# Rows of a mixture of experts: products with selection matrices, or indirect transfers through memory

## The chip, the core and the metric

The kernel runs on one core of one Trainium2 chip. The metric is device microseconds from start to end of one execution; where several executions are given, their median. TensorE (PE) multiplies, VectorE (DVE) and ScalarE (ACT) work elementwise, GpSimd (POOL) does a little of both, and SyncE (SP) only issues transfers between memory (DRAM) and the on-chip SBUF. Each engine has a queue of its own that it works through in order; semaphores hold an instruction until what it needs has been done. Results of TensorE lie in PSUM.

## What is computed

Two layers on 256 tokens of width 1024: layer 0 is a state-space mixer with memory attention and a dense gated feed-forward, layer 1 an RWKV mixer with memory attention and then the experts, to which the change belongs. Of the reference only these lines matter (8 experts, each token goes to the 2 best, 3584 feed-forward columns an expert):

```python
logits = (hf @ w_router).astype(f32) + b_router.astype(f32)
top_logit, top_idx = lax.top_k(logits, TOP_K)
top_w = jax.nn.softmax(top_logit, axis=-1)
...
xb = hf[row_tok].reshape(n_blocks, MOE_BLOCK, d)
def expert_block(args):
    xblk, e = args
    return swiglu(xblk, w_gate[e], w_up[e], w_down[e])
yb = lax.map(expert_block, (xb, block_expert)).reshape(n_rows, d)
yb = yb * row_w[:, None].astype(yb.dtype)
out = jnp.zeros_like(hf).at[row_tok].add(yb)
```

So each expert takes the rows of its tokens, runs silu(x·gate) · (x·up) through down, and its rows are weighted and added to the tokens that they came from.

## The kernel before

**Precision.** Every large product is made of three fp32r products (`mm3`, L191 to L195): a matrix is split into a high part (ScalarE casts it, `wsh`, L187) and a residual (VectorE subtracts, `wsl`, L188); the same goes for the other factor (`xeh` and `xel`, `ath` and `atl`).

**Experts.** `experts` (L1709) runs 8 experts × 7 chunks of 512 feed-forward columns. A chunk loads three weight pieces of 2 MB (gate, up, down) on SyncE's queue into a ring of 7 buffers. `split` cuts each into 4 pieces of 128x1024; high parts and residuals go through rings of 4. `gate_up` (L1636) makes 24 products of 128x512 for gate and 24 for up into PSUM tiles `gu`, then `sg`: silu on ScalarE (L1649), times up on VectorE (L1650). `act_T` (L1653) turns sg with four transposes into a PSUM tile `t` and splits it into ath (L1658) and atl (L1659). `down` adds 24 products to the expert's sums `yac`. The tiles `t` share a ring of two PSUM buffers, whether sg, an expert's rows or the small products of `back` stand in them:

```python
def tr():
    return pp.tile([P, 4, P], F32, name="t", tag="tr", bufs=2)
def gu():
    return pp.tile([P, 512], F32, name="gu", tag="gu", bufs=4)
```

**Gather and return.** An expert has at most 128 rows here. `Gm` (L1454) is a 0/1 matrix, tokens by places. `rows` multiplies it with the normalised tokens `xhp` (high and low: eight products, L1458); ScalarE copies the result (`xr`, L1465), eight transposes put it in columns (L1468), and `xeh`, `xel` (L1470, L1471) are its parts. `back` (L1476) transposes Gm (L1478), gets each row's weight with two small products (L1480) and copies both. After the last chunk of an expert, `combine` (L1677) scales yac by the weight (yeh on ScalarE, L1685; yel on VectorE, L1686), returns the rows by eight products with the transposed Gm (L1691, L1692) and adds to `xs` (L1696). A gather is written behind chunk 3 of the expert before it, a return between gate and up of chunk 1 of the next. The last return ends the kernel together with the final norm. A second pass for experts with more than 128 rows stands in the program behind a branch and isn't entered here.

**Order.** A scheduler sets the order of the instructions on each engine when the program is built; on the chip each engine keeps to it.

**Elsewhere.** At the start SyncE loads the tokens, the first projection weights and the small matrices of the state-space mixer, `bnat` and `cnat` among them. Before the experts, the router (`xg`, L1570, GpSimd multiplies tokens by the norm's gain into one of two buffers) makes xhp, and `wt`, for each token and expert its weight and its norm factor.

## Time and profile before

| | us |
|---|---|
| median of 3 runs (1590.15 to 1592.48) | 1592.29 |
| the profiled execution | 1590.0 |
| its span | 1588.0 |
| TensorE busy in the span | 1516.3 (95%) |
| VectorE busy | 1283.0 (81%) |
| ScalarE busy | 1073.0 (68%) |
| GpSimd busy | 157.7 (10%) |

The experts take the stretch from about 590 to 1575 us; all that stands before them (two mixers, the dense feed-forward, the router) takes the first 590. Shares over the whole span mix these. The trace can be asked for a stretch (how long each engine is busy in it, at which granted clock of TensorE, at which share of the transfer engines), for lines (how often, how long, what ended the idle time before), and for single instructions in order of time. In such a row the arrow in brackets names the instruction whose end released the one shown, with the idle time ahead of it. PEld is the weight load of TensorE, which runs beside its products. Products overlap, so the price of one is the distance to the next, not the duration in its row.

### The profile page before, as it was taken

To read this page: it belongs to the slowest core of one execution; us is meant where nothing else is said; L and a number is where in the kernel's file an instruction comes from. 1 tells how busy PE (TensorE), PEld (TensorE's weight loads), DVE (VectorE), ACT (ScalarE), POOL (GpSimd) and SP (SyncE) were. 2 spreads that over 40 slices of the span, in tenths; PEclk is the share of its full clock that TensorE was granted. 3 is DMA by queue.
4 is the path that set the end of the run, shared out by engine and by line. 5 is a ranking of instruction groups with operands and counts; after the bars stand their busy time and mean duration, and the time that the engine had idled before them with its cause. 6 is when DMAs were issued, how large, how long until landed. Compare 5 with 4: busy or idle time off the path is not lost. (4 is left out here: it accounts for less than half of the span.)

```text
span 1588.0 us, 21853 instructions
## 1 busy us (share of the span) xinstructions
PE 1516.3 (95%) x8465; PEld 1272.1 (80%) x8465; DVE 1283.0 (81%) x1583; ACT 1073.0 (68%) x1355; POOL 157.7 (10%) x215
## 2 busy tenths in 40 slices
PE   7898999998969889999999999999999999999996
PEld 6776888878958768888888888888888888888885
DVE  7964654546895669899899899899899898988987
ACT  6655544436533348788777777787787887777775
POOL 3451000003652230000000000000000000000000
PEclk9999999999989979999999999999999999999999
DMA  7116553623400958999999999999999999999970
GB/s 202 45 45 237 185 203 117 248 79 94 120 14 22 339 218 313 341 371 359 346 374 353 344 376 356 340 378 356 347 372 363 348 366 361 352 348 366 360 280 29
DMA packets 198031, 423.46 MB, mean 267 GB/s; under 512 B 13952, under 2 KB 35614, under 8 KB 197918
## 3 DMA queue, kind: packets, MB, share of 16 engines
q1 hardware_dynamic: 195746, 419.29, 72.8%
q10 hardware_dynamic: 2172, 2.68, 0.6%
q8 instruction: 68, 1.11, 0.3%
q14 instruction: 45, 0.37, 0.1%
HBM read 420.91 MB, written 1.05 MB: 266 GB/s over the span
## 5 line engine op out<-in xcount | busy, mean ns | idle before, releaser
L188 DVE TENSOR_TENSOR wsl<-w,wsh 128x1024 fp32r<-128x1024 f32 (+1 forms) x757 | 893.8, 1216 | 150.9 <-ACT wsh L187 139.8
L187 ACT CAST wsh<-w 128x1024 fp32r<-128x1024 f32 (+1 forms) x757 | 783.3, 1049 | 250.9 <-PE gu L195 97.1
L194 PE MATMUL gu<-wsl,xeh 128*128 128x512 f32 x896 | 350.7, 391 | 0.0
L193 PE MATMUL gu<-wsh,xeh 128*128 128x512 f32 x896 | 348.9, 396 | 1.6 <-DVE xs L1696 1.6
L195 PE MATMUL gu<-wsh,xel 128*128 128x512 f32 x896 | 349.5, 390 | 0.0
L193 PEld LDWEIGHTS gu<-wsh,xeh 128*128 128x128 f32 x896 | 168.8, 188 | 37.4 <-ACT wsh L187 2.4
L195 PEld LDWEIGHTS gu<-wsh,xel 128*128 128x128 f32 x896 | 168.6, 188 | 35.1 <-DVE xel L1471 0.2
L194 PEld LDWEIGHTS gu<-wsl,xeh 128*128 128x128 f32 x896 | 168.7, 188 | 35.0
L194 PE MATMUL yac<-wsl,ath 128*128 128x512 f32 x440 | 173.0, 393 | 0.0
L195 PE MATMUL yac<-wsh,atl 128*128 128x512 f32 x440 | 171.7, 390 | 0.0
L193 PE MATMUL yac<-wsh,ath 128*128 128x512 f32 x440 | 136.3, 391 | 0.0
L278 POOL TENSOR_TENSOR rs<-vv,mhalf 128x1 f32<-128x1 f32 x8 | 4.4, 557 | 1203.6 <-DVE vv L277 1203.6
L195 PEld LDWEIGHTS yac<-wsh,atl 128*128 128x128 f32 x440 | 82.7, 188 | 17.1
L193 PEld LDWEIGHTS yac<-wsh,ath 128*128 128x128 f32 x440 | 82.2, 188 | 16.9
L194 PEld LDWEIGHTS yac<-wsl,ath 128*128 128x128 f32 x440 | 82.8, 188 | 15.4
L193 PE MATMUL mm<-wsh,hTh 128*128 128x512 f32 (+1 forms) x192 | 71.1, 374 | 0.0
L194 PE MATMUL mm<-wsl,hTh 128*128 128x512 f32 (+1 forms) x192 | 70.8, 371 | 0.0
L195 PE MATMUL mm<-wsh,hTl 128*128 128x512 f32 (+1 forms) x192 | 70.3, 372 | 0.0
L1658 ACT CAST ath<-t 128x512 fp32r<-128x512 f32 x55 | 32.3, 587 | 31.0 <-PE yac L194 30.2
L1650 DVE TENSOR_TENSOR sg<-sg,gu 128x512 f32<-128x512 f32 x56 | 38.1, 681 | 13.7 <-PE gu L195 13.7
L195 PE MATMUL dn<-hTh,wsC 128*128 128x256 f32 x160 | 46.5, 291 | 1.0 <-POOL wsC L1148 0.9
L193 PE MATMUL dn<-hTh,wsC 128*128 128x256 f32 x160 | 46.1, 288 | 0.0
(533 smaller groups left out, 2059.1 us busy)
## 6 DMA issues: line engine op xcount, KB each, us to landing
w<-in_moe_w_gate_dram SPq DMA_DIRECT2D x55, 2048.0 KB
...
```

The source lines that it names most:

```text
L187: S.copy(hv, src)
L188: (eng or V).tensor_sub(lv, src, hv.bitcast(F32))
L193: TE.matmul(ps, xp[0], wh, start=start, stop=False, skip_group_check=True)
L194: TE.matmul(ps, xp[0], wl, start=False, stop=False, skip_group_check=True)
L195: TE.matmul(ps, xp[1], wh, start=False, stop=stop, skip_group_check=True)
L278: hold.append(G.tensor_tensor(rs, vv, mhalf, op=OP.pow).ins)
L1650: V.tensor_mul(sg, sg, ps[1])
L1658: S.copy(at[0], t)
```

## The change

Two buffers in memory are added: `xd`, the 256 tokens' rows, and `yd`, two rows of results for each token. yd is filled with zeros at the start by four writes of 512 KB on SyncE. The router writes each of the four xg to xd (256 KB each). `wt` gets two more columns, the token's number and the number of its row in yd (a token's first expert writes the first half, its second one the second; where the token isn't the expert's, the number lies outside).

For experts 1 to 7 `found` replaces `gather`, one chunk earlier: Gm, the two small products (now four columns: weight, norm factor, token, place), two conversions to integers (`it`), and an indirect transfer on GpSimd's queue that fetches 128 rows of 4 KB from xd into the tile `ye`, of which there is one. Behind chunk 3 the transposes take their rows from ye. For experts 0 to 6 `combine` scales yac into ye (two operations on ScalarE) and an indirect transfer on GpSimd's queue writes the rows to their places in yd; places outside are skipped. In the last expert, behind chunks 2 to 5, `added` loads a quarter of yd into ye (512 KB on SyncE) and VectorE adds it to xs (128x1024). The first expert's gather and the last one's return stay products.

```diff
     consts = pool(ctx, "consts", 1)
-    pad(consts, 64)
     sml = pool(ctx, "sml", 2)
...
     ring = {}
+    dr = pool(ctx, "dr", 1, space=bass.MemoryType.DRAM)
+    xd = dr.tile([T, D], F32, name="xd")
+    yd = dr.tile([2 * T, D], F32, name="yd")
     keep_st = ctx.enter_context(ExitStack())
...
             dma(srow2[:, j, :], a[nm][0].rearrange("(q g) j -> q (g j)", g=8))
+        for i in range(2 * NH):
+            dma(yd[i * P:(i + 1) * P, :], KD_[:, 0:2].rearrange("p q d c -> p (q d c)"))
         bnat = su.tile([P, 2, NST, 16], F32, name="bnat", tag="n1")
...
     xhp = mkpair(mcon, [P, NH, D], "xhp")
-    wt = mcon.tile([P, NH, E, 2], F32, name="wt")
+    wt = mcon.tile([P, NH, E, 4], F32, name="wt")
+    tok = mcon.tile([P, NH], F32, name="tok")
     rs3 = mcon.tile([P, NH], F32, name="rs3")
...
     cmi = mcon.tile([P, 1], I32, name="cmi")
+    pad(mcon, 96)
...
             self.Gm = self.mp.tile([P, NH, P], F32R, name="Gm")
-            self.pg = [pg() for _ in range(2)]
+            self.pg = pg and [pg() for _ in range(2)]
...
                 x_ = xr(q)
-                (V.tensor_copy if q and xrV else S.copy)(x_, self.pg[q])
+                if self.pg:
+                    (V.tensor_copy if q and xrV else S.copy)(x_, self.pg[q])
                 t = self.tr()
...
-        def back(self, tr):
-            self.GT = self.mp.tile([P, NH, P], F32R, name="GT")
+        def back(self, tr, turned):
             t, e = tr(), self.e
+            if turned:
+                self.GT = self.mp.tile([P, NH, P], F32R, name="GT")
+                for h in range(NH):
+                    TE.transpose(t[:, h, :], self.Gm[:, h, :].bitcast(F32), ident)
             for h in range(NH):
-                TE.transpose(t[:, h, :], self.Gm[:, h, :].bitcast(F32), ident)
-            for h in range(NH):
-                TE.matmul(t[:, 2, 0:2], self.Gm[:, h, :].bitcast(F32), wt[:, h, e, :], start=h == 0, stop=h == NH - 1,
+                TE.matmul(t[:, 2, 0:4], self.Gm[:, h, :].bitcast(F32), wt[:, h, e, :], start=h == 0, stop=h == NH - 1,
                           skip_group_check=True)
-            S.copy(self.GT, t[:, 0:2, :])
+            if turned:
+                S.copy(self.GT, t[:, 0:2, :])
             wsl = smk([P, 2], F32, "wsl")
...
             self.w, self.rs = wsl[:, 0:1], wsl[:, 1:2]
+            it = smk([P, 2], I32, "it")
+            V.tensor_copy(it[:, 0:1], t[:, 2, 2:3])
+            V.tensor_scalar(it[:, 1:2], t[:, 2, 3:4], 2.0 * T, None, op0=OP.add)
+            self.row, self.place = it[:, 0:1], it[:, 1:2]
+        def find(self, tr, rows):
+            for h in range(NH):
+                V.tensor_scalar(self.Gm[:, h, :], iot, float(self.base), posm[:, h, self.e:self.e + 1], op0=OP.add,
+                                op1=OP.is_equal)
+            self.back(tr, self.e == E - 1)
+            G.indirect_dma_start(rows, None, xd[:, :], bass.IndirectOffsetOnAxis(self.row, 0))
...
         dma(gain, bass.AP(tensor=ap.tensor, offset=ap.offset + D, ap=[[0, P], [1, D]]), S)
+        G.iota(tok, pattern=[[P, NH]], base=0, channel_multiplier=1, allow_small_or_imprecise_dtypes=True)
         G.iota(iot, pattern=[[1, P]], base=0, channel_multiplier=0, allow_small_or_imprecise_dtypes=True)
...
             G.tensor_mul(xg, xs[:, h, ns], gain[:, ns])
+            dma(xd[h * P:(h + 1) * P, ns], xg)
             S.copy(xhp[0][:, h, ns], xg)
...
         V.tensor_copy(wt[:, :, :, 1], rs3[:, :, None].to_broadcast([P, NH, E]))
+        V.tensor_copy(wt[:, :, :, 2], tok[:, :, None].to_broadcast([P, NH, E]))
+        V.tensor_scalar(wt[:, :, :, 3], rkk, float(T), -2.0 * T, op0=OP.mult, op1=OP.add)
+        V.tensor_add(wt[:, :, :, 3], wt[:, :, :, 3], wt[:, :, :, 2])
...
+    def ye_tile():
+        return mp.tile([P, D], F32R, name="ye", tag="ye", bufs=1)
+    def halved(t):
+        return lambda q: t[:, q * 512:(q + 1) * 512].bitcast(F32)
     def gather(e, base):
...
             g.rows(h)
-        g.columns(lambda q: mp.tile([P, 512], F32R, name="xr", tag="ye" + "hl"[q], bufs=1).bitcast(F32))
-        g.back(tr)
+        g.columns(halved(ye_tile()))
+        g.back(tr, True)
         return g
+    def found(e):
+        g = Gather(e, 0, None, tr)
+        g.ye = ye_tile()
+        g.find(tr, g.ye.bitcast(F32))
+        return g
+    def added(k, h):
+        b = ye_tile().bitcast(F32)
+        dma(b, yd[k * T + h * P:k * T + (h + 1) * P, :])
+        V.tensor_add(xs[:, h, :], xs[:, h, :], b)
...
-    def combine(yac, g, last):
+    def combine(yac, g, last, base):
...
         ys = [None, None]
+        if not (base or last):
+            y = ye_tile().bitcast(F32)
+            for n in range(2):
+                S.activation(y[:, n * 512:(n + 1) * 512], yac[n], AF.Copy, scale=g.w)
+            G.indirect_dma_start(yd[:, :], bass.IndirectOffsetOnAxis(g.place, 0), y, None, bounds_check=2 * T - 1,
+                                 oob_is_err=False)
+            return
...
         def scaled(n):
-            yh, yl = ys[n] = mkpair(mp, [P, 512], "ye", 1) if n == 0 or not last else mkpair(mp, [P, 4, P], "at", 1)
+            if n == 0 or not last:
+                y = ye_tile()
+                yh, yl = ys[n] = y[:, 0:512], y[:, 512:D]
+            else:
+                yh, yl = ys[n] = mkpair(mp, [P, 4, P], "at", 1)
             if len(yh.shape) > 2:
...
                 if first:
-                    info[0].back(tr)
+                    info[0].back(tr, False)
                 if pend:
...
                     e_ = done.pop()
-                    combine(yacs[e_], info[e_], False)
+                    combine(yacs[e_], info[e_], False, base)
             sg = gate_up(info[e], w_in, between, base + e + c == 0)
...
                 at = act_T(sg, mps[e % 2 ^ 1])
-            if c == 3 and e + 1 < E:
+            if e + 1 < E and not base:
+                if c == 2:
+                    info[e + 1] = found(e + 1)
+                if c == 3:
+                    info[e + 1].columns(halved(info[e + 1].ye))
+            elif c == 3 and e + 1 < E:
                 info[e + 1] = gather(e + 1, base)
+            if e == E - 1 and not base and 2 <= c < 2 + 2 * NH:
+                added((c - 2) // NH, (c - 2) % NH)
             if pend:
...
         finish(pend, at, w_down(*pend[:2], 4))
-        combine(yacs[E - 1], info[E - 1], True)
+        combine(yacs[E - 1], info[E - 1], True, base)
```

**The order around an expert's rows.** TensorE's queue before, where expert 3 gets its rows (gu_7940 is the up product of the running chunk, xr the fetched rows):

```order
L194 MATMUL gu_7940<-wsl_7962,xeh_6949 128x512
L195 MATMUL gu_7940<-wsh_7961,xel_6950 128x512
L1468 MATMUL t_8001<-ident_76,xr_7999 128x128
L1468 MATMUL t_8010<-ident_76,xr_8008 128x128 x3
L193 MATMUL gu_7940<-wsh_7971,xeh_6949 128x512
L1468 MATMUL t_8010<-ident_76,xr_8008 128x128
```

And TensorE's queue in the changed kernel at the same expert (its lines: L195 to L197 mm3, L1475 the transposes of ye, L1700 those of sg; gu_8063 is the up product, behind 48 products of gate and up):

```order
L196 MATMUL gu_8063<-wsl_8095,xeh_6934 128x512
L197 MATMUL gu_8063<-wsh_8094,xel_6935 128x512
L1475 MATMUL t_7953<-ident_79,ye_7799 128x128 x4
L1475 MATMUL t_7960<-ident_79,ye_7799 128x128 x4
L1700 MATMUL t_8054<-ident_79,sg_7948 128x128 x4
L1700 MATMUL t_8194<-ident_79,sg_8104 128x128 x4
L195 MATMUL yac_7656<-wsh_8107,ath_8059 128x512
L196 MATMUL yac_7656<-wsl_8108,ath_8059 128x512
```

The transposes of the rows stood among products; now four groups of four stand together, in two PSUM buffers, with no product between them, and the down products need the third group. The same rows stand at experts 4 to 7.

VectorE's queue before, in the same place:

```order
L188 TENSOR_TENSOR wsl_8047<-w_7888,wsh_8046 128x1024
L1471 TENSOR_TENSOR xel_7998<-t_8001,xeh_7997 128x512
L1650 TENSOR_TENSOR sg_7981<-sg_7981,gu_7940 128x512
L1471 TENSOR_TENSOR xel_7998<-t_8010,xeh_7997 128x512
L188 TENSOR_TENSOR wsl_8057<-w_7888,wsh_8056 128x1024
```

VectorE's queue in the changed kernel (L190 the residual, L1694 sg, L1478 xel, L1703 atl):

```order
L190 TENSOR_TENSOR wsl_8108<-w_8011,wsh_8107 128x1024
L1694 TENSOR_TENSOR sg_8104<-sg_8104,gu_8063 128x512
L190 TENSOR_TENSOR wsl_8118<-w_8011,wsh_8117 128x1024
L190 TENSOR_TENSOR wsl_8128<-w_8011,wsh_8127 128x1024
L190 TENSOR_TENSOR wsl_8138<-w_8011,wsh_8137 128x1024
L1478 TENSOR_TENSOR xel_7952<-t_7953,xeh_7951 128x512
L1478 TENSOR_TENSOR xel_7952<-t_7960,xeh_7951 128x512
L1703 TENSOR_TENSOR atl_8060<-t_8054,ath_8059 128x512
```

The two xel, one of which stood ahead of sg and one right behind it, now stand behind sg and three residuals.

VectorE's queue at the end of the changed kernel, from the last sg on (L1678 are the additions of yd, L1741 the last return's residuals; in the queue before, these L1678 rows are not there and the rest stands alike):

```order
L1694 TENSOR_TENSOR sg_13465<-sg_13465,gu_13424 128x512
L1678 TENSOR_TENSOR xs_75<-xs_75,ye_13030 128x1024
L190 TENSOR_TENSOR wsl_13508<-w_13369,wsh_13507 128x1024
L190 TENSOR_TENSOR wsl_13523<-w_13517,wsh_13522 128x1024
L190 TENSOR_TENSOR wsl_13527<-w_13517,wsh_13526 128x1024
L1703 TENSOR_TENSOR xel_13474<-t_13468,xeh_13473 128x512
L190 TENSOR_TENSOR wsl_13531<-w_13517,wsh_13530 128x1024
L190 TENSOR_TENSOR wsl_13535<-w_13517,wsh_13534 128x1024
L1678 TENSOR_TENSOR xs_75<-xs_75,ye_13173 128x1024
L1741 SCALAR_TENSOR_TENSOR atl_13566<-yac_12746,wsl_11877,ath_13565 128x512
L1678 TENSOR_TENSOR xs_75<-xs_75,ye_13316 128x1024
L1741 SCALAR_TENSOR_TENSOR ye_13562<-yac_12745,wsl_11877,ye_13562 128x512
```

Three of the four additions stand behind the last sg; the tile ye of the last one and of the last return's first half is the same memory.

## Rows read from the trace of the kernel before

**Rows 1.** Stretches (us): busy time (instructions) of PE, PEld, DVE, ACT, POOL; clock, DMA share, GB/s.
```profile
4.00:20.00 16.00, 10.71 (x63) 9.96 (x64) 13.47 (x83) 7.76 (x15) 5.83 (x17) 1.00 1.02 250
1000.00:1025.00 25.00, 25.00 (x121) 20.75 (x120) 21.57 (x22) 19.59 (x23) 0.00 (x0) 1.00 0.91 330
1500.00:1525.00 25.00, 25.00 (x114) 20.72 (x113) 22.64 (x22) 20.79 (x22) 0.00 (x0) 1.00 0.99 357
1525.00:1550.00 25.00, 25.00 (x116) 20.72 (x115) 21.60 (x21) 19.55 (x20) 0.00 (x0) 1.00 0.57 221
```

**Rows 2.** Waits of SyncE's queue: line, awaited work, us in total, times, longest.
```profile
SPq L63 <- DVE wsl L188: 1034.2, 178, 26.2
```

**Rows 3.** Timeline (start, duration): first gather product's load of experts 1 and 2; two chunks' silu.
```profile
641.63 0.19 PEld L1458 LDWEIGHTS gu<-xhph,Gm 128*128 128x128 f32 x1
...
664.38 0.68 ACT L1649 ACTIVATE sg<-gu,wsl 128x512 f32<-128x512 f32 x1
...
681.16 0.68 ACT L1649 ACTIVATE sg<-gu,wsl 128x512 f32<-128x512 f32 x1
...
764.61 0.19 PEld L1458 LDWEIGHTS gu<-xhph,Gm 128*128 128x128 f32 x1
```

**Rows 4.** Timeline: first and last gather product of expert 2, its two transposes, its weights.
```profile
764.83 0.39 PE L1458 MATMUL gu<-xhph,Gm 128*128 128x512 f32 x1
...
766.41 0.39 PE L1458 MATMUL gu<-xhpl,Gm 128*128 128x512 f32 x1
...
778.02 0.38 PE L1478 MATMUL t<-ident,Gm 128*128 128x128 f32 x2
...
778.24 0.50 PE L1480 MATMUL t<-wt,Gm 128*128 128x2 f32 x4
```

**Rows 5.** Lines from 590 to 1575 us: count, busy us, mean ns, idle before.
```profile
L1458 PE MATMUL gu<-xhph,Gm 128*128 128x512 f32 x28 | 10.9, 389 | 0.0
...
L1691 PE MATMUL gu<-yeh,GT 128*128 128x512 f32 x30 | 9.8, 393 | 0.3 <-ACT yeh L1685 0.3
```

**Rows 6.** Timeline behind a chunk's last up product, and the same stretch's lines for ath, xel.
```profile
1527.78 0.69 DVE L1650 TENSOR_TENSOR sg<-sg,gu 128x512 f32<-128x512 f32 x1 [1.61 <-PE gu L195]
1527.78 1.06 ACT L187 CAST wsh<-w 128x1024 fp32r<-128x1024 f32 x1 [0.30 <-PE gu L195]
...
1528.39 6.90 DVE L188 TENSOR_TENSOR wsl<-w,wsh 128x1024 fp32r<-128x1024 f32 x6
...
L1658 ACT CAST ath<-t 128x512 fp32r<-128x512 f32 x55 | 32.3, 587 | 31.0 <-PE yac L194 30.2
...
L1471 DVE TENSOR_TENSOR xel<-t,xeh 128x512 fp32r<-128x512 f32 x14 | 9.6, 683 | 0.0
```

**Rows 7.** Timeline of the last chunk and the last return on VectorE and ScalarE.
```profile
1562.24 0.68 DVE L1650 TENSOR_TENSOR sg<-sg,gu 128x512 f32<-128x512 f32 x1
1562.91 4.84 DVE L188 TENSOR_TENSOR wsl<-w,wsh 128x1024 fp32r<-128x1024 f32 x4
...
1572.83 0.69 ACT L1685 ACTIVATE yeh<-yac,wsl 128x512 fp32r<-128x512 f32 x1 [4.52 <-PE yac L195]
...
1573.56 0.75 DVE L1686 SCALAR_TENSOR_TENSOR yel<-yac,wsl,yeh 128x512 fp32r<-128x512 f32 x1 [3.98 <-ACT yeh L1685]
```

**Rows 8.** Timeline: TensorE after two idles; stretches around them, columns as in rows 1.
```profile
43.42 0.66 PE L568 MATMUL trp<-ident,BC 128*128 128x128 f32 x4 [4.44 <-ACT BT L569]
...
543.98 0.45 PE L1372 MATMUL rw<-ident,ysq 128*128 128x128 f32 x1 [4.07 <-DVE ysq L1369]
...
44.00:48.00 4.00, 4.00 (x90) 3.16 (x90) 4.00 (x15) 1.76 (x3) 3.57 (x11) 0.57 0.00 0
...
540.00:545.00 5.00, 1.02 (x4) 1.04 (x5) 4.49 (x9) 4.38 (x6) 2.35 (x3) 0.74 0.87 229
545.00:550.00 5.00, 5.00 (x14) 3.86 (x13) 2.80 (x3) 0.37 (x1) 0.12 (x1) 0.57 1.02 380
```

**Rows 9.** Timeline at the start: two loads of 512 KB, and the first use.
```profile
0.81 0.88 SPq L63 DMA_DIRECT2D xs<-in_x_dram  x2
...
4.76 1.06 ACT L162 ACTIVATE xh<-xs 128x1024 f32<-128x1024 f32 x1 [1.78 <-DMA xs<-in_x_dram]
```

## The prediction

> **What bounds the kernel now.** The page's shares are means over stages with different limits, so the first view that I argue from is the table of stretches [rows 1]. Of the 25 us from 1000 on, TensorE is busy all 25.00 at granted clock 1.00, VectorE 21.57 and ScalarE 19.59; the DMA share is 0.91 at 330 GB/s. From 1525 to 1550 TensorE is still at 25.00 though the DMA share has sunk to 0.57: the loads are ahead, and what they wait for is a ring buffer that VectorE must release (178 waits of SyncE's queue on its residual, [rows 2]). So from 590 to 1575 us TensorE's own queue sets the time, and what the change does to it counts in full.
>
> Is it bound by issue, or by small waits inside the 25.00? A plain chunk takes 681.16 − 664.38 = 16.78 us, an expert 764.61 − 641.63 = 122.98 us [rows 3]. Seven chunks are 117.5 us, which leaves 5.5 us for gather and return. The gather's eight products stand 1.58 us apart from first to last, 0.226 us each; two transposes of Gm take 778.24 − 778.02 = 0.22 us, 0.11 each [rows 4]. Sixteen products and ten transposes are 3.6 + 1.1 = 4.7 us, so 0.8 us are left for the two small weight products and everything else: TensorE doesn't wait for gather or return in the kernel before. Its price is its issue time.
>
> **What is taken off TensorE.** Experts 1 to 7 lose eight gather products each, experts 0 to 6 eight return products each (in the stretch of the experts 28 of the gather's records are there for each half of the pair, [rows 5], so seven experts' worth, and 30 for the first half of the returned pair): 112 × 0.226 = 25.3 us. Of eight pairs of Gm transposes only the last expert's stays: 7 × 0.22 = 1.5 us. The eight transposes into columns stay. Together −26.8 us. The ScalarE copies, VectorE residuals and xs additions that go with them lie beside a full TensorE and are worth nothing by themselves.
>
> **What is put on TensorE's path: five stalls.** This is the term that decides. At experts 3 to 7 the order puts the transposes of ye directly behind 48 gate and up products, then the transposes of two chunks' sg, then the down products. The transposes share two PSUM buffers (t). The first four and second four take both; the third group needs the first back, and it is free only when VectorE has done xel of it. In VectorE's order xel stands behind sg of the chunk that has just ended and three residuals. Call the end of the up products zero. The sg multiplication starts 0.30 later (ScalarE's release by the same product is 0.30) and takes 0.61 to 0.69; residuals follow each other at 6.90 / 6 = 1.15 us, 1.21 at the end of the kernel; xel is 0.68 [rows 6, 7]. That is 0.30 + 0.65 + 3 × 1.18 + 0.68 = 5.2 us, between 5.0 and 5.3. Then come the sg transposes (4 × 0.11 = 0.45), the cast ath (0.59, [rows 6]), and two hand-overs of about 0.2: the down products start at 6.5. TensorE has sixteen transposes to do in that time, 1.8 us, so it idles 4.7 us, and nothing gives it back since it has no slack afterwards. Five places: +23.5 us. In the kernel before, the xr transposes stand among up products and only one chunk's sg is open there, so this wait isn't in the trace; the bounds are 4.4 and 5.1 us a place, from the bounds of the chain.
>
> At expert 1 there are some 73 products (16 us) between the index products and the ye transposes, at expert 2 some 95 with the transposes between gate products; I count no stall there.
>
> **The clock.** Each of those stalls has one unbroken idle of about 4.2 us (from 1.0 to 5.2). In the trace TensorE's idles of 4.44 and 4.07 us are followed by stretches at a granted clock of 0.57 [rows 8], that is, mostly the 1.2 GHz level: (1 − 0.57) × 4 = 1.7 us and (1 − 0.57) × 5 = 2.2 us lost. But there TensorE was also thinly used ahead of them (1.02 of the 5 us from 540 on); here it is full on both sides. From 0 to 2.2 us each; I take that half the places pay 2 us: +5 us, 0 to 11.
>
> **The end of the kernel.** Four additions of yd (128x1024, VectorE, by the residual of the same size 1.2 us) enter the last expert. The first falls into VectorE's wait for sg (1.61 us, [rows 6]) and costs nothing. The second stands between the last sg and the last five residuals, a stretch in which VectorE runs without a gap from 1562.24 [rows 7]: +1.2. The fourth needs a load that SyncE can issue only when the third has been done (all use the single ye buffer). Two 512 KB loads issued at 0.81 us have the first in use at 4.76 [rows 9]: 3.5 to 4 us for one. ScalarE's scaling of the last product, which started at 1572.83 [rows 7], writes the same buffer and so waits for the fourth addition. By the chain (third addition 1571.9, load 1575.7, addition 1576.9, scaling and residual 1578.4, against 1574.3 before) the end moves +3 to +5; I take +4.
>
> **The start.** Four 512 KB writes of zeros into yd are queued on SyncE ahead of bnat, cnat and the next projection weights. The row of 4 to 20 us shows 1.02 DMA share at 250 GB/s; 2 MB at the 250 to 357 GB/s of [rows 1] are 5.9 to 8.4 us of a queue that is full. TensorE's idle of 4.44 us before 43.42 [rows 8] ends on ScalarE's BT and not on a load, and swallows up to that much of what delays TensorE ahead of it. 0 to +8 us; I take +2, nearer to the lower end for that idle.
>
> **The router.** Each xg is now also written to memory behind weight loads, and xg has two buffers, so the third and fourth may wait for the first write: a 2 MB weight load ahead of it is 5.5 us at the 380 GB/s of [rows 8], of which I allow half on the path. 0 to +3, I take +1; the small tok and place operations are in that.
>
> **Gather and return themselves.** No row shows a transfer issued by GpSimd, nor an indirect one. As a transfer of 512 KB the nearest row is again the load of at most 4 us [rows 9]; as a share of traffic 1 MB per expert beside 44 MB (357 GB/s for 123 us) is 2.4%, with buffers already waiting [rows 2]. Lower end: nothing, since 16 us (expert 1) and about 31 us (later ones; the index conversion stands two chunks ahead) cover it. Upper end: it takes its turn behind all that is outstanding in the weight ring: six 2.1 MB buffers at 357 GB/s [rows 1] are 35 us, 19 too late once and 4 too late six times, +43 us. I take nothing, by the row of the single load.
>
> The Trainium skill, "SBUF — State Buffer", the section on the DMA port ("The 'DVE blocks DMA' trap"), speaks against moving transfers to GpSimd's queue: there the descriptors are written by GpSimd, and a VectorE operation in a two-port mode, such as an fp32 copy inside SBUF, locks it out until it ends. VectorE is busy 21.57 of 25 us here, but with tensor-tensor residuals; the same page's "Who interferes with whom" says these have no such mode and hold only the read port. By the first rule the gathers come late, by the second not; no run so far shows which.
>
> **The sum** against the profiled run of 1590.0 (its span of 1588.0 and 2.0 around it): −26.8 + 23.5 + 5 + 4 + 2 + 1 = +8.7, 1598.7. The median of the runs is 2.3 above the profiled one, so 1601; I write 1600.
>
> **The rivals.**
> *No clock loss.* All as above but the clock stays up at all five places: 1600 − 5 = 1595, 1592 to 1598 with the other bounds. For it: full use on both sides of each idle. Against: both idles of [rows 8] that are as long did lose.
> *Clock loss at every place and the upper ends at start and router:* 5 × 2.2 instead of 5, +6; start and router up to +6 more: 1606 to 1612.
> *Faster: the stalls are short.* One mechanism: the third group of transposes doesn't wait for xel, because what VectorE does between zero and xel overlaps with TensorE's work (it is later than VectorE's queue). Without stalls and clock loss: 1592.3 − 26.8 + 7 = 1572.5. It decides the sign when a place costs less than (26.8 − 7 − 3.2) / 5 = 3.3 us. For it: VectorE gains some slack from the work removed. Against: sg waits for the last up product by data, and order is fixed behind it.
> *Gathers late.* With four loads outstanding, 8.4 MB at 357 GB/s = 23 us, expert 1 waits 7 us: 1607; with six, 1643. A GpSimd held off by VectorE ends in the same rows. Against it: SyncE waits for buffers, so few loads are queued at a time.
>
> **Chances.** Forecast (1595.5 to 1605) 0.48; no clock loss 0.20; loss everywhere 0.10; gathers late 0.09; short stalls 0.13. Range: from 1586 (halfway into the short stalls, a chance of 0.07 below) to 1612 (late gathers, 0.08 above). A measurement of this kernel can tell about 0.2%, 3.2 us. Slower by more: forecast, full loss, late gathers and a little of the second, 0.68; within: most of the second and a piece of the short stalls, 0.20; faster: 0.12.
>
> **What would show it.** Right: five idles of TensorE of 4 to 5 us, once per expert from the third on, each ended by xel or by ath; the five periods with a stall about 1 us longer than 122.98, or 3 us with the clock lost, those without one some 4 us shorter; an end about 4 us later. Wrong: TensorE waits ended by the GpSimd transfer; no idle at the five places; a start later by more than 6 us.

## The result, and the profile after

The changed kernel takes 1607.77 us in the median of four runs (1606.40 to 1610.20), against 1592.38 for the kernel before beside it: 1.0095 times as long, with an interval of 1.0082 to 1.0109. It is slower by 15 us, where +8 had been forecast; the time lies in the range, but above the forecast's own bounds of 1595.5 to 1605. The profiled execution is the slowest of the four, 1610.2 with a span of 1607.9, that is 19.9 more than the span of before, whose profiled execution (1590.0) is faster than all four of its runs. All shifts below are against the profiled execution of before, so they add up to these 19.9, 4.5 more than the medians differ by.

The page of the kernel after: busy time and share of the span by engine, then groups (count, busy us, mean ns, idle before), and transfers (count, us from issue to landing).

```profile
PE 1506.2 (94%) x8339; PEld 1264.6 (79%) x8339; DVE 1271.6 (79%) x1564; ACT 1060.6 (66%) x1332; POOL 171.5 (11%) x230
...
q0 software_dynamic: 2016, 5.51, 0.9%
...
L1700 PE MATMUL t<-ident,sg 128*128 128x128 f32 x224 | 36.7, 295 | 19.6 <-DVE xel L1478 19.6
...
ye<-xd,it POOLq DMA_INDIRECT x7, 7.8
yd<-ye,it POOLq DMA_INDIRECT x7, 8.3
```

TensorE is busy 10 us less than before and yet the kernel is longer. The group L1700 says where to look: 19.6 us in which TensorE had nothing to do ahead of the transposes of sg, all of it ended by VectorE's xel. The indirect transfers are not the place: landed 8 us after issue, 0.9% of the transfer engines, and no idle of TensorE ends on one of them.

Following one instruction that both kernels have (silu, once in each of the 56 chunks) gives the shift by stage:

| stage | shift at its end | of which here | forecast |
|---|---|---|---|
| start, up to the first product with w_out (141.78 before, 150.03 after) | +8.3 | +8.3 | +2 |
| both mixers and the feed-forward | +8.5 | +0.2 | 0 |
| router | +12.4 | +3.8 | +1 |
| experts | +16.0 | +3.6 | −26.8 + 28.5 = +1.7 |
| end | +19.9 | +3.9 | +4 |

**The experts.** Expert 1 to expert 2 takes 118.97 us from first silu to first silu, against 122.97 in the kernel before: −4.0, with no stall. The next five periods are 1.67, 2.46, 2.82, 3.51 and 2.62 us longer than the same periods before. Against −4.0, each holds a stall: 5.7, 6.5, 6.8, 7.5 and 6.6, together 33.1. The timeline of one of these places, the kernel after, TensorE, VectorE, ScalarE (start, duration, engine, line, work, in brackets the idle time and what ended it):

```profile
1039.76 0.39 PE L197 MATMUL gu<-wsh,xel 128*128 128x512 f32 x1
1039.99 1.03 PE L1475 MATMUL t<-ident,ye 128*128 128x128 f32 x8
...
1040.19 0.69 DVE L1694 TENSOR_TENSOR sg<-sg,gu 128x512 f32<-128x512 f32 x1 [1.61 <-PE gu L197]
1040.80 3.49 DVE L190 TENSOR_TENSOR wsl<-w,wsh 128x1024 fp32r<-128x1024 f32 x3
...
1044.20 1.28 DVE L1478 TENSOR_TENSOR xel<-t,xeh 128x512 fp32r<-128x512 f32 x2
...
1044.94 1.31 PE L1700 MATMUL t<-ident,sg 128*128 128x128 f32 x8 [3.91 <-DVE xel L1478]
1045.63 0.58 ACT L1702 CAST ath<-t 128x512 fp32r<-128x512 f32 x1 [3.43 <-PE t L1700]
...
1046.27 0.80 PE L195 MATMUL yac<-wsh,ath 128*128 128x512 f32 x1
```

The ye transposes are done at 1041.02 and both buffers of t are full. The third group waits until 1044.94 for the first xel, which stands behind sg and three residuals in VectorE's queue. The first down product starts 6.28 us after the up products have been issued; the prediction's chain said 6.5. The wait of 3.91 is there five times, ended by xel each time: at 919.87, 1044.94, 1169.94, 1296.18 and 1422.71. At the four other places the eight transposes behind it take 1.97 us instead of 1.31, since the granted clock has fallen ahead of them, and the first down product starts 6.73 or 6.74 us after the up products.

What stands behind it costs too. Stretches of the kernel after around two of the five places (columns as in [rows 1]: busy time of PE, PEld, DVE, ACT, POOL, then granted clock, DMA share, GB/s):

```profile
1036.00:1040.00 4.00, 4.00 (x20) 3.25 (x19) 2.29 (x2) 3.44 (x4) 0.00 (x0) 1.00 1.05 387
1040.00:1045.00 5.00, 1.09 (x10) 0.85 (x9) 4.81 (x6) 2.02 (x3) 0.00 (x0) 1.00 1.01 401
1045.00:1047.00 2.00, 1.98 (x10) 1.41 (x11) 1.18 (x2) 0.58 (x1) 0.00 (x0) 0.75 0.87 294
1047.00:1049.00 2.00, 2.00 (x7) 1.52 (x5) 0.00 (x0) 0.00 (x0) 0.00 (x0) 0.50 1.05 409
1049.00:1051.00 2.00, 2.00 (x9) 1.64 (x8) 0.68 (x1) 1.26 (x2) 0.00 (x0) 0.90 1.05 409
...
1170.00:1172.00 2.00, 2.00 (x9) 1.78 (x10) 0.77 (x2) 0.58 (x1) 0.00 (x0) 0.50 0.84 261
1172.00:1174.00 2.00, 2.00 (x5) 1.55 (x6) 0.40 (x1) 0.00 (x0) 0.00 (x0) 0.50 1.02 393
1174.00:1176.00 2.00, 2.00 (x7) 1.54 (x6) 0.23 (x1) 1.04 (x1) 0.00 (x0) 0.57 1.05 410
```

TensorE is full and at 1.00 (2.4 GHz) up to the stall, sits idle 3.9 us, and comes back at 0.50 (1.2 GHz) for a while: in the stretches shown (1 − 0.75) × 2 + 0.50 × 2 + (1 − 0.90) × 2 = 1.7 us are lost at the one place, 1 + 1 + 0.86 = 2.9 at the other. The clock fell at all five. In the 8 us from the first down product on it is 0.91, 0.80, 0.75, 0.75 and 0.76, which by (1 − clock) × 8 is 8.2 us in all.

**The start.** Timeline of the kernel after, SyncE's issues (three of the four writes of zeros stand in the first row) and the waits behind them:

```profile
6.84 1.95 SPq L63 DMA_DIRECT2D yd<-KD  x3
...
15.18 1.68 SPq L63 DMA_DIRECT2D cnat<-in_s_c_re_dram  x1
...
45.67 0.94 PE L572 MATMUL trp<-ident,BC 128*128 128x128 f32 x4 [4.84 <-ACT BT L573]
...
74.93 1.97 PE L559 MATMUL trp<-ident,xh 128*128 128x128 f32 x8 [6.56 <-ACT xh L554]
...
148.93 2.94 ACT L189 CAST wsh<-w 128x1024 fp32r<-128x1024 f32 x3 [3.64 <-DMA w<-in_w_out_dram]
150.03 1.22 PE L195 MATMUL mm<-wsh,cath 128*128 128x512 f32 x2 [6.15 <-ACT wsh L189]
```

cnat was issued at 9.97 before. The idle that was to swallow the delay ([rows 8], 4.44) has become 4.84 and starts 2 us later; then the transposes of the second half of the memory, which waited 0.42 before, wait 6.56, and ScalarE's cast of w_out waits 3.64 for its load instead of 1.31. One idle did not swallow the lateness of a queue that feeds everything behind it. Not all of the +8.3 is the writes': in eight other profiled executions with the same writes at the start the w_out product is 4.7 to 8.7 us late, and in three without them there (the experiments that write the zeros in the RWKV mixer) it is still 1.3 to 3.9 us late.

**The end.** The last two additions of yd in VectorE's timeline of the kernel after; the load for the second of them is issued at 1587.51, when the first is done:

```profile
1586.27 1.22 DVE L1678 TENSOR_TENSOR xs<-xs,ye 128x1024 f32<-128x1024 f32 x1
...
1590.83 1.23 DVE L1678 TENSOR_TENSOR xs<-xs,ye 128x1024 f32<-128x1024 f32 x1 [0.36 <-DMA ye<-yd]
```

### The profile page after: what moved, and what is told of

It is laid out like the page before. It is cut to its first block, busy times and chain, and to the rows that moved or that the text cites. A ratio compares the mean times of both kernels' runs of the same rounds, so it can differ in the third digit from the quotient of the medians.

```text
span 1607.9 us, 21635 instructions
## 1 busy us (share of the span) xinstructions
PE 1506.2 (94%) x8339; PEld 1264.6 (79%) x8339; DVE 1271.6 (79%) x1564; ACT 1060.6 (66%) x1332; POOL 171.5 (11%) x230
## 5 line engine op out<-in xcount | busy, mean ns | idle before, releaser
L190 DVE TENSOR_TENSOR wsl<-w,wsh 128x1024 fp32r<-128x1024 f32 (+1 forms) x757 | 896.8, 1216 | 159.9 <-ACT wsh L189 145.7
L197 PE MATMUL gu<-wsh,xel 128*128 128x512 f32 x896 | 349.8, 390 | 0.0
L195 PE MATMUL gu<-wsh,xeh 128*128 128x512 f32 x896 | 348.2, 395 | 0.0
L197 PEld LDWEIGHTS gu<-wsh,xel 128*128 128x128 f32 x896 | 168.7, 188 | 35.4 <-DVE xel L1478 0.2
L195 PEld LDWEIGHTS gu<-wsh,xeh 128*128 128x128 f32 x896 | 168.8, 189 | 33.9 <-ACT xeh L1477 0.2
L197 PE MATMUL yac<-wsh,atl 128*128 128x512 f32 x440 | 173.2, 396 | 0.0
L195 PE MATMUL yac<-wsh,ath 128*128 128x512 f32 x440 | 143.2, 399 | 0.0
L195 PEld LDWEIGHTS yac<-wsh,ath 128*128 128x128 f32 x440 | 84.8, 193 | 19.0 <-ACT ath L1702 1.2
L197 PEld LDWEIGHTS yac<-wsh,atl 128*128 128x128 f32 x440 | 84.3, 191 | 18.0
L1728 POOL DMA_INDIRECT yd<-ye,it x7 | 8.9, 1269 | 678.0 <-ACT ye L1727 678.0
L195 PE MATMUL mm<-wsh,hTh 128*128 128x512 f32 (+1 forms) x192 | 71.1, 374 | 0.0
L197 PE MATMUL mm<-wsh,hTl 128*128 128x512 f32 (+1 forms) x192 | 70.7, 372 | 0.0
L1700 PE MATMUL t<-ident,sg 128*128 128x128 f32 x224 | 36.7, 295 | 19.6 <-DVE xel L1478 19.6
L1694 DVE TENSOR_TENSOR sg<-sg,gu 128x512 f32<-128x512 f32 x56 | 38.2, 682 | 18.9 <-PE gu L197 18.9
L1700 PEld LDWEIGHTS t<-ident,sg 128*128 128x128 f32 x224 | 30.0, 152 | 26.8 <-DVE xel L1478 20.9
```

The costliest lines, as they stand in the source:

```text
L190: (eng or V).tensor_sub(lv, src, hv.bitcast(F32))
L195: TE.matmul(ps, xp[0], wh, start=start, stop=False, skip_group_check=True)
L197: TE.matmul(ps, xp[1], wh, start=False, stop=stop, skip_group_check=True)
L1694: V.tensor_mul(sg, sg, ps[1])
L1700: TE.transpose(t[:, j, :], sg[:, j * P:(j + 1) * P], ident)
L1728: G.indirect_dma_start(yd[:, :], bass.IndirectOffsetOnAxis(g.place, 0), y, None, bounds_check=2 * T - 1, oob_is_err=False)
```

## Experiments

Every run was timed beside the kernel before (1591.5 to 1592.3 in the median). "Shift" is again that of the profiled execution.

**Columns behind chunk 5.** The transposes of the fetched rows are written two chunks later; all else stays.

```diff
-                if c == 3:
+                if c == 5:
                     info[e + 1].columns(halved(info[e + 1].ye))
```

> The transposes of the fetched rows are written behind chunk 5 of the expert before instead of chunk 3; nothing else changes. Theory: in the changed kernel the five idles of 3.91 us that xel ends, with the half-level clock behind them, cost 5.7 to 7.5 us each, 33 us in all, and are a matter of where these transposes stand. With two more chunks ahead of them the order spreads them among products, so the time falls by about 33 us, to 1575, below the kernel before. Rival: VectorE's sg and residuals hold the transposes' buffers wherever they stand, the idle moves with them and the time stays above 1600. A second rival, that the indirect fetch itself is late, would also give a gain here, but the fetches landed a median of 7.8 us after their issue, about 140 us of wait less than it would need.

Measured: 1586.37 in the median of ten executions, ratio 0.9978 (0.9946 to 1.0010), 21 us less than the changed kernel. Seven lie from 1581.63 to 1587.40, two at 1599.30 and 1602.17, and one took 8481.5, which nothing on record explains. What follows is the profiled one, 1584.31. Every stall has gone, there is no idle of 1.5 us or more in TensorE among the experts, and the granted clock stays at 1.00 there. So stall and clock loss come from that place in the order. It misses the expected 1575 by 11 us. The five periods are shorter than before by 4.2, 2.2, 2.1, 1.9 and 2.7, not by 4: at the new place ScalarE casts the second half's xeh in front of a weight cast and waits for TensorE. Timeline of this kernel:

```profile
1042.56 0.59 ACT L1477 CAST xeh<-t 128x512 fp32r<-128x512 f32 x1 [3.44 <-PE t L1475]
...
1044.14 0.51 PE L195 MATMUL gu<-wsh,xeh 128*128 128x512 f32 x1 [0.47 <-ACT wsh L189]
1045.40 0.50 PE L196 MATMUL gu<-wsl,xeh 128*128 128x512 f32 x1 [0.75 <-DVE wsl L190]
```

Some 2 us at four of the places, 7 us in all, is a second and smaller stall of the same kind, on ScalarE's queue; it is gone in the two last versions below, where the two halves stand in different chunks. The rest is the end, 6.7 us late here instead of 3.9.

**TensorE kept busy in the stall.** The wait and the clock cannot be told apart by removing the stall, so here the second group of transposes is issued six times. The order on ScalarE doesn't change, and on VectorE only neighbours swap at a few places; but TensorE's does: at experts 4 to 7 the last four transposes of sg now stand behind the first four down products.

```diff
-                for j in range(4):
+                for j in [0, 1, 2, 3] * (6 if q and self.e > 2 and not self.pg else 1):
                     TE.transpose(t[:, j, :], x_[:, j * P:(j + 1) * P], ident)
```

> The changed kernel, but at experts 3 to 7 the second group of the fetched rows' transposes is issued six times over (20 transposes more at each place, about 2.2 us of TensorE, the same values into the same PSUM buffer). The order on VectorE and ScalarE is the same as in the changed kernel, and the chain that ends the stall (sg, three residuals, xel) is not longer. Theory: the wait itself is 4.7 us a place whatever TensorE does in it, and the rest of the 33.1 us, some 9.6 us, is the granted clock lost to the idle of 3.9 us; with the idle cut to about 1.7 us the clock stays up and the time falls to about 1598 to 1602, though work was added. Rival one: the clock falls anyway, or the extra 1 to 3 us a place is not the clock: 1607 to 1609, each stall as long as before. Rival two: the transposes are not hidden behind the wait: 5 x 2.2 more, 1619.

Measured: 1603.18, ratio 1.0067 (1.0048 to 1.0087). The idle is cut from 3.91 to 1.73, and at experts 4 to 7, where the last four transposes have moved, a second one of 0.68 follows. Timeline at expert 5, then stretches around expert 4's place and expert 5's, of this kernel:

```profile
1160.75 3.22 PE L1475 MATMUL t<-ident,ye 128*128 128x128 f32 x28
...
1164.96 1.28 DVE L1478 TENSOR_TENSOR xel<-t,xeh 128x512 fp32r<-128x512 f32 x2
...
1165.70 0.66 PE L1700 MATMUL t<-ident,sg 128*128 128x128 f32 x4 [1.73 <-DVE xel L1478]
...
1167.03 0.50 PE L195 MATMUL yac<-wsh,ath 128*128 128x512 f32 x1 [0.68 <-ACT ath L1702]
...
1168.09 0.60 PE L1700 MATMUL t<-ident,sg 128*128 128x128 f32 x4
```

```profile
1041.00:1043.00 2.00, 1.55 (x5) 1.17 (x6) 0.69 (x1) 0.40 (x1) 0.00 (x0) 0.76 0.96 333
1043.00:1045.00 2.00, 2.00 (x9) 1.71 (x8) 0.00 (x0) 0.21 (x1) 0.00 (x0) 0.50 1.02 393
...
1166.00:1168.00 2.00, 1.32 (x8) 0.93 (x7) 0.93 (x2) 0.59 (x1) 0.00 (x0) 1.00 0.90 249
1168.00:1170.00 2.00, 2.00 (x13) 1.64 (x11) 0.00 (x0) 0.81 (x1) 0.00 (x0) 1.00 1.05 407
```

From the transposes' start to the first down product it is 6.28 us, as in the changed kernel, though 2.2 us of TensorE's work were added: the wait is VectorE's chain. The clock fell all the same at four of the five places (0.50 from 1043 on) and stayed at 1.00 at one, expert 5. That one place separates the two: its period is 1.04 longer than before, so its stall is 1.04 + 4.0 = 5.0 us without any clock loss. Of these, 0.35 are the four transposes that moved behind the wait (1168.09 to the next product at 1168.44); in the changed kernel they lie inside it. The wait there is then 5 × 4.7 = 23.5 us, and the clock the other 33.1 − 23.5 = 9.6 us. The granted clock of the changed kernel agrees: 8.2 us from the first down products on, and four times 0.46 (6.74 − 6.28) ahead of them, 10.0 in all. The split rests on one place without clock loss. My theory had the clock stay up everywhere; on that, the rival was right at four places. The work added was transposes alone; whether products in the wait would have kept the clock up was not tried. This kernel is 4.6 us faster in the median and 7.1 in the profiled execution. Of that the experts give 2.2; most of the rest is a profiled execution that reached the experts 5 us earlier (+5.3 at the w_out product instead of +8.3), with the same program up to there, so it proves nothing.

**Only the return by transfer.** All experts get their rows by products again (`if c == 3 and e + 1 < E: info[e + 1] = gather(e + 1, base)`, no `found`); results go back through yd, and Gm is transposed for the last expert alone.

> Half of the change: the results go back by indirect transfers, as in the changed kernel, but all experts get their rows by gather products and keep the order of the kernel before there. Theory: the whole of the slowdown is the fetching half. TensorE loses 56 return products and seven pairs of transposes, 56 x 0.226 + 7 x 0.22 = 14.2 us; the start costs 5.6 to 8.3, the router 3.8, the end 4; no idle of TensorE over 1.5 us among the experts: 1592.3 - 14.2 + 13.4 to 16.1 = 1591.5 to 1594. Rival: the tile ye that the return shares, or GpSimd's writes, stall TensorE too: above 1600.

Measured: 1590.70, ratio 0.9999 (0.9984 to 1.0013); the ten runs lie from 1589.18 to 1592.94 but for one of 1600.22. No idle of 1.5 us among the experts; they are 16.0 us shorter (forecast 14.2), start and router cost 9.9 and the end 7. So the returning half pays about what its surroundings cost, and the fetching half by itself makes the loss: +3.6 instead of −16.0 in the experts.

**The zeros alone, added to the kernel before.**

```diff
             dma(srow2[:, j, :], a[nm][0].rearrange("(q g) j -> q (g j)", g=8))
+        for i in range(2 * NH):
+            dma(yd[i * P:(i + 1) * P, :], KD_[:, 0:2].rearrange("p q d c -> p (q d c)"))
```

> The kernel before with one thing added: the four 512 KB writes of zeros on SyncE's queue at the start, ahead of bnat, cnat and the next projection weights. Theory: the start's cost of the change is these writes alone and is never given back: 1592.3 + 5.6 to 8.3 = 1598 to 1600.5. Rival: the start's cost comes from the other edits there (constants laid out elsewhere, SBUF addresses moved): 1592 to 1593.

Measured: 1596.31 (1595.17 to 1598.35, ten runs), ratio 1.0020 (1.0010 to 1.0031): +4.0 in the median. In the profiled execution the w_out product comes at 147.23, +5.5, and from 601 us to the last chunk the shift stays between +6.98 and +7.14: nothing gives it back. The writes alone do it, a little cheaper than expected; the rival, other edits at the start, falls.

**The zeros later, and elsewhere.** First from a tile of zeros of their own, behind the projections' loads (yd written at 71 us instead of 7):

```diff
-        for i in range(2 * NH):
-            dma(yd[i * P:(i + 1) * P, :], KD_[:, 0:2].rearrange("p q d c -> p (q d c)"))
...
+        zero = wk.tile([P, D], F32, name="zero", tag="xh", bufs=2)
+        G.memset(zero, 0.0)
+        for i in range(2 * NH):
+            dma(yd[i * P:(i + 1) * P, :], zero)
```

> The four 512 KB writes of zeros into yd leave the start; they are written behind the projections' loads and the memory rows, from a tile of zeros of their own. Theory: the changed kernel is 8.3 us late by 150 us because these 2 MB stand ahead of bnat, cnat and the projection weights in the one queue; the time falls by about 8 us, to 1599.5. Rival: the start is late since the order of its work was laid out anew (the second load of memory rows stands 14 us later), and the writes cost what they cost wherever they are: within 2 us of 1607.8.

Measured: 1607.67 (1602.37 to 1614.86), ratio 1.0108 (1.0069 to 1.0147), the same as the changed kernel. The w_out product is still +5.1 late (146.85), so it is not the place among the first 20 us alone that makes the writes dear; at 71 us, still ahead of w_out's load, they cost as much. Then from the RWKV mixer, on ScalarE's queue (the first at 377 us, where the transfer engines of the kernel before are busy to a share of 0.36, from 370 to 400 us):

```diff
-        for i in range(2 * NH):
-            dma(yd[i * P:(i + 1) * P, :], KD_[:, 0:2].rearrange("p q d c -> p (q d c)"))
...
         G.memset(Nt[:, 24:, :], 0.0)
+        for i in range(2 * NH):
+            dma(yd[i * P:(i + 1) * P, :], Nt[:, 24:, :].rearrange("p u t -> p (u t)"), S)
```

> The zeros of yd are written in the RWKV mixer of layer 1 (420 to 500 us, where the transfers stand nearly idle), from a zeroed part of a tile that is there anyway, issued by ScalarE's queue; SyncE's queue at the start is that of the kernel before. Theory: the 2 MB at the start cost 5 to 8 us in whatever place they stand there (moved behind the projections they still left the kernel 5.1 us late at 147 us); in a quiet stretch they cost nothing, TensorE reaches the layer-0 output projection at 142 us as before, and the time is 8 us (5.5 us against the other runs of the same start) below the changed kernel's 1607.8: 1600 to 1602. Rival: the later start comes from the order that the scheduler makes of the start as a whole, whether or not the writes are there: unchanged.

Measured: seven runs in two groups, three from 1601.79 to 1601.98, three from 1614.19 to 1616.91, one of 1606.38; ratio 1.0095 (1.0060 to 1.0130). In the profiled execution (1614.19) the start was +3.0 at the w_out product and still +2.8 at 364 us, 5 to 6 better than the changed kernel, as expected, and lost about 12 us later, in a stretch of the mixer that has small products. Its stretches:

```profile
485.00:495.00 10.00, 10.00 (x147) 7.92 (x146) 3.78 (x8) 3.56 (x8) 5.95 (x5) 0.50 0.01 2
495.00:505.00 10.00, 10.00 (x86) 7.98 (x84) 3.39 (x6) 0.27 (x1) 0.00 (x0) 0.50 0.01 2
505.00:515.00 10.00, 10.00 (x65) 9.51 (x64) 2.66 (x7) 4.06 (x11) 0.70 (x1) 0.54 0.30 79
```

In the last experiment below, with the same edit, the profile shows 0.83, 1.00, 1.00 and 1.00 from 480 to 520, and in the kernel before 0.83, 1.00, 1.00 and 1.00. Why some executions of this variant stay at the lower level there is open; TensorE was counted busy all 10 us of each row in both cases. Only one execution was profiled; the mean granted clock of the others fits (0.966 in the lower group, 0.955 and 0.956 in the two others of the upper one). The lower group is the expected 1600 to 1602.

**xd written by GpSimd's queue.** The forecast's reason for the router was that the writes land late behind weight loads.

```diff
-            dma(xd[h * P:(h + 1) * P, ns], xg)
+            dma(xd[h * P:(h + 1) * P, ns], xg, G)
```

> The four writes of xg into xd are issued from GpSimd's queue instead of SyncE's. Theory: the router's 3.4 to 3.8 us come from the second xg, which waits for its buffer until the first one's write has landed behind 8 MB of weights on SyncE's queue; the time falls by 3.5 us, to 1604.3. Rival: the small added operations on VectorE (tok, place) are what is late: unchanged, 1607.8.

Measured: 1611.39 (1609.55 to 1619.75), ratio 1.0140 (1.0105 to 1.0175), not better: from the last products with ysq (552.53 in the changed kernel) to the product of sel behind the router's longest wait (596.33) the router takes 44.9 us, against 43.8 in the changed kernel and 40.0 before. The landing isn't the cause: the second xg waits for TensorE's logits here too. The end is 7.2 us late here instead of 3.9, which has nothing to do with the router (see the end, below).

**xd written from the high part.** xd gets xhp's high part instead of xg, so xg has no reader more than before; the fetched rows of experts 1 to 7 lack their residual here.

```diff
-            dma(xd[h * P:(h + 1) * P, ns], xg)
             S.copy(xhp[0][:, h, ns], xg)
+            dma(xd[h * P:(h + 1) * P, ns], xhp[0][:, h, ns].bitcast(F32))
```

> xd is written from xhp's high part, a tile that stays, and not from xg; this leaves the residual out of the rows that experts 1 to 7 fetch. Theory: the router's 3.8 us come from xg's two buffers, which xg shares with h3: with the write as one more reader of xg the order puts the second xg behind two more logit groups, and xhpl, the logits and the second half's additions follow it on VectorE; without that reader the order is that of the kernel before, and the time falls by 3.8 us to 1604. Rival: the transfers themselves, or the added small operations of the router, are what is late; then nothing changes, as when the writes went by GpSimd's queue.

Measured: the router is back at 39.99 us (39.98 before), so the 3.8 us come from reading xg. What it changes is the second xg on GpSimd. The kernel after:

```profile
577.33 1.30 POOL L1592 TENSOR_TENSOR xg<-xs,gain 128x512 f32<-128x512 f32 x1 [14.17 <-PE pr L1560]
```

and this one:

```profile
570.33 1.31 POOL L1592 TENSOR_TENSOR xg<-xs,gain 128x512 f32<-128x512 f32 x1 [9.67 <-PE pr L1560]
```

xg shares its two buffers with the router's transposed rows h; with one more reader of xg the scheduler sets the second xg behind later logit products, and it waits 14.17 instead of 9.67 us, both times for a logit product (pr). The whole kernel took 1608.18 all the same (1607.30 to 1608.82; ratio 1.0106, 1.0085 to 1.0128), since its end came 7.2 us late instead of 4: the last two additions waited 2.21 and 3.09 us for their loads, in another order of VectorE (see the end, below).

**Three additions early.** Three parts of yd are loaded at chunk 1 of the last expert into three tiles, by GpSimd's queue, and added there by VectorE; one is left for the end.

```diff
...
+        for j in range(3):
+            dma(bs[j], yd[j * P:(j + 1) * P, :], G)
+        for j in range(3):
+            V.tensor_add(xs[:, j % 2, :], xs[:, j % 2, :], bs[j])
...
```

> The four quarters of yd are loaded by GpSimd's queue into three tiles (two of the idle pair of columns, and ye), three of them in one go behind chunk 1 of the last expert, so that three additions stand before the last chunks, one in the last, and none waits for a load at the end nor shares a buffer with the last return. Theory: the end of the changed kernel is 3.9 us later than before, 2.4 us of it the second and third addition and the rest the wait for the last load; one addition of 1.2 us stays: 2.7 us less, 1605.1. Rival: VectorE has no room for three additions around chunk 4, TensorE waits for residuals there and the time is unchanged or longer.

Measured: 1611.89 (1610.64 to 1623.80), ratio 1.0150 (1.0105 to 1.0196), slower. From the last silu to the first store of the result it is 27.1 us (before 25.7, changed kernel 29.8), so the end does get shorter by 2.6; but chunks 5 and 6 of the last expert lose 0.7 and 4.1 us. Timeline of this kernel at the second of them:

```profile
1557.24 0.69 ACT L1700 ACTIVATE sg<-gu,wsl 128x512 f32<-128x512 f32 x1 [5.79 <-PE gu L197]
...
1558.91 0.50 PE L195 MATMUL gu<-wsh,xeh 128*128 128x512 f32 x1 [1.71 <-ACT wsh L189]
```

TensorE waits for a cast that stands behind silu in ScalarE's queue, and silu has waited 5.79 us for TensorE. That is ScalarE's order and not a lack of room on VectorE: the same wait of 1.71 is in the two kernels below whose additions are on GpSimd (at 1559.45 and 1524.12). So the rival is not shown; at most the 0.7 us of chunk 5 are VectorE's.

**The additions on GpSimd.**

```diff
...
-        V.tensor_add(xs[:, h, :], xs[:, h, :], b)
...
+                G.tensor_add(xs[:, h, :], xs[:, h, :], b)
```

(with the tiles and loads of two parts at a time, from chunk 1 on.)

> All four additions of yd go to GpSimd, their loads to its queue, in the two idle tiles of columns. Theory: VectorE has 1.3 us to spare in a chunk and three additions there cost 5 us in the run with three tiles; on GpSimd, idle in the last expert, they cost TensorE nothing, and the end, which was 3.9 us late, is as before: 1604. Rival: GpSimd's additions hold VectorE off. At 576 us of the kernel before three GpSimd subtractions of 128x1024 take 7.03 us, and VectorE's operations of 64 columns take 2.26 to 2.38 us beside them instead of 0.23. If the residuals of a chunk wait like that, four additions of 2.3 us cost up to 9 us less four times 1.3: 1608 or a little more.

Measured: 1612.36 (1610.92 to 1612.90), ratio 1.0129 (1.0107 to 1.0151). The end is only 1.1 late, but chunk 3 costs 5.2 and chunk 6 4.0; the latter is ScalarE's order again, long after the last addition (1517.5). Timeline of this kernel at chunk 3, VectorE, GpSimd and the product that waits; the first row holds four residuals:

```profile
1498.26 9.06 DVE L190 TENSOR_TENSOR wsl<-w,wsh 128x1024 fp32r<-128x1024 f32 x4 [0.26 <-ACT wsh L189]
1498.74 3.02 POOL L1683 TENSOR_TENSOR xs<-xs,xeh 128x1024 f32<-128x1024 f32 x1 [6.10 <-DMA xeh<-yd]
1501.72 3.38 POOL L1683 TENSOR_TENSOR xs<-xs,xel 128x1024 f32<-128x1024 f32 x1
...
1506.24 0.50 PE L196 MATMUL gu<-wsl,xeh 128*128 128x512 f32 x1 [1.68 <-DVE wsl L190]
```

The four residuals take 9.06 us: the first and the last 1.2 each, as elsewhere, and the two that run beside GpSimd's additions 3.44 and 3.42. The rival was right on the mechanism. The Trainium skill, "SBUF — State Buffer", section "Who interferes with whom", says that a VectorE operation with two inputs in SBUF contends with a GpSimd operation that reads SBUF; this trace agrees, with 3.44 against 1.2 us.

**Two versions that put it together.** Both write the zeros in the mixer and the first half of the columns behind chunk 5, the second behind chunk 6; the first has the additions on GpSimd as well, the second leaves them on VectorE.

```diff
...
-                if c == 3:
-                    info[e + 1].columns(halved(info[e + 1].ye))
+                if c in (5, 6):
+                    info[e + 1].columns(halved(info[e + 1].ye), qs=(c - 5,))
...
```

> Zeros in the RWKV mixer, additions on GpSimd, and the transposes of the fetched rows one half behind chunk 5 and one behind chunk 6, so that in TensorE's queue the two halves stand in different chunks. Theory: the parts are independent and add up: 1607.8 - 8.3 - 33 - 3.9 = 1563, 29 us below the kernel before, which is the 28 us of products and transposes taken off TensorE, with the router's 3.8 us left. Rival: with the five stalls gone another wait comes to the front, as with the columns behind chunk 5, where ScalarE's cast for the second half held up the weights' high parts for 2 us an expert: 1575 to 1580.

Measured: 1580.98 (1573.20 to 1591.45, ten runs), ratio 0.9940 (0.9916 to 0.9964). It misses the expected 1563 by 18. At the last expert's third chunk the profiled execution was 22.2 us ahead of the kernel before; by the last chunk it had lost 10, 4.6 of them beside GpSimd's additions and 5.6 in the last chunk, with the wait of 1.71 behind ScalarE's cast.

> The changed kernel with two edits: the transposes of the fetched rows stand one half behind chunk 5 and one half behind chunk 6 (no stall), and the zeros are written in the RWKV mixer; the four additions stay on VectorE. Theory: the run with the additions on GpSimd was 22 us ahead of the kernel before at the last expert's third chunk and lost 10 us there; with VectorE's additions the loss is the end's 4 to 7 us alone: 1592.3 - 22 + 4 to 7 = 1574 to 1577. Rival: VectorE has no room for them in the last expert, as where three of them stood early: 1580 or more. A stretch of the RWKV mixer at the lower clock level, seen in some executions of the other two kernels with this edit, would put some 10 us on an execution under either theory.

Measured: 1581.61 (1573.79 to 1584.52, six runs), ratio 0.9930 (0.9910 to 0.9950). The profiled execution, 1573.79, is what was expected, but the median misses it by 5 us: two of the six are of that kind and four above 1581. The mean granted clock is 0.972 and 0.973 in the two and 0.965 to 0.968 in the four, as between the two groups of the zeros in the RWKV mixer; where the four lost it was not profiled. By the last chunk it was 24.1 us ahead; the experts alone went from +5.35 to −24.10, that is −29.5 without a stall. The end gives 7.9 back. Its timeline:

```profile
1548.61 1.22 DVE L1679 TENSOR_TENSOR xs<-xs,ye 128x1024 f32<-128x1024 f32 x1 [2.08 <-DMA ye<-yd]
...
1553.30 1.23 DVE L1679 TENSOR_TENSOR xs<-xs,ye 128x1024 f32<-128x1024 f32 x1 [2.65 <-DMA ye<-yd]
1554.56 0.69 ACT L1741 ACTIVATE ye<-yac,wsl 128x512 fp32r<-128x512 f32 x1 [4.69 <-DVE xs L1679]
...
1555.30 0.79 PE L1747 MATMUL gu<-ye,GT 128*128 128x512 f32 x1 [6.16 <-ACT ye L1741]
```

Both versions beat both kernels, the one before by 0.6 to 0.7%; the two can't be told from each other.

## Why the prediction was right, and where it wasn't

The direction and the mechanism were right: TensorE's queue sets the time, the removed products count in full, and five stalls take it back. The size was short by 11 us in the sum over the profiled executions (+8.7 forecast, +19.9 measured) and by 7 in the medians, which rose by 15.4. That the time still lies in the range owes something to luck: its upper end, 1612, was set by late gathers, which did not come. Of the signs named, the five idles of 3.91 ended by xel, the longer and shorter periods and the later end came; so did one of the signs of being wrong, a start more than 6 us late (8.3 in this execution). Term by term:

| term | forecast | measured | by |
|---|---|---|---|
| products and transposes removed | −26.8 | −29.5 | the experts of the last version, which have no stall |
| five waits | +23.5 | +23.5 | the place without clock loss, 4.7 each |
| clock behind them | +5 (0 to 11) | +9.6 | 33.1 − 23.5 |
| end | +4 (3 to 5) | +3.9 | shift; 3.9 to 4.3 in three other kernels, 6.7 to 7.9 in five |
| start | +2 (0 to 8) | +8.3 | shift; 4.7 to 8.7 in other executions of the same writes, +4.0 in the median of the zeros alone |
| router | +1 (0 to 3) | +3.8 | 43.8 − 40.0 us |

- **Removal.** Each expert gains 4.0 us where the working made it 16 × 0.226 + 0.22 = 3.8. What else went from the queues was "worth nothing by itself" in the working; the small difference may be what it was worth. No run took it apart.
- **The waits.** The chain of VectorE (sg, three residuals, xel) was sized within 0.3 us: 6.5 to the first down product forecast, 6.28 measured where the clock was still up. That the wait is this chain and not TensorE's own work is shown by the kernel with 20 more transposes in it, which has the same 6.28; that it hangs on the place alone, by the one with the columns behind chunk 5.
- **The clock.** I let half of the places pay 2 us, because TensorE was full on both sides here, unlike [rows 8]. All five paid, 1.9 on average. Full use on both sides was no protection, and with an idle of 1.73 instead of 3.91, filled with transposes, the clock still fell at four places of five. What decides at the fifth isn't known.
- **The start** is the term that was most wrong in the profiled execution, and the failed step is the choice of the lower end "for that idle". The bounds from the bytes, 5.9 to 8.4 us, were nearer to what was measured (4.0 for the zeros alone, 4.7 to 8.7 in nine profiled executions). The working looked at the one idle that hid a delay and not at what the same queue delivers after it: the second part of the memory (idle 0.42 to 6.56) and w_out (1.31 to 3.64).
- **The router** was sized too low and for a wrong reason: the landing of the writes isn't it (GpSimd's queue doesn't help), the extra reader of a shared pair of buffers is, by way of the order. That could be read in the order of the changed kernel before any run.
- **The end** followed the written chain step by step: third addition 1586.27, load issued 1587.51, fourth addition 1590.83, scaling 1592.09. The load took 3.3 us, against the 3.5 to 4 of [rows 9]. In five other kernels (columns behind chunk 5, the return alone, the two with xd written otherwise, and the last version) the end cost 6.7 to 7.9 us. The loads are not slower there (3.2 to 3.8 us from issue to addition); VectorE's order is another. The first addition behind the last sg starts 6.0 us behind it, after four residuals and xel (as those stand in the kernel before; the changed kernel has xel behind three, so its queue is not quite the one before with additions put in), instead of 0.6, and the next one comes so soon after it that it too waits for its load, 2.1 to 2.3 us. So the +4 holds for the order that was read, and the order at the end changed with edits elsewhere.
- **Gather and return** cost TensorE nothing, as assumed by the row of a single load: the fetches landed in 5.0 to 8.7 us, and their first transpose came 14.6 (expert 1) to 30.6 us after their issue, though the DMA share beside them is 1.00 and not 0.91 (1000 to 1025 us). Of the two rules of the Trainium skill's "SBUF — State Buffer" that were weighed, the one on tensor-tensor operations ("Who interferes with whom") agrees: GpSimd's 14 indirect instructions took 1.25 us each on average beside a VectorE that is busy 21.48 of 25 us with residuals, and no idle of TensorE ended on one of their transfers. The lock-out of the Trainium skill's "The 'DVE blocks DMA' trap" (the same page) shows nowhere here, but all except 8 us of VectorE's work from 600 to 1573 us is tensor-tensor, so it was not put to the test.

Of the rivals the one with the full clock loss and the upper ends at start and router, 1606 to 1612, is what came; it had a chance of 0.10. Its three parts were added as if they were unlikely together, while each of them had an argument of its own for the upper end.
